# Modulation vectors in 512-column pieces, summed in fp32 straight from their accumulators, with layer 0's MLP gate row made inside the MLP

## The chip, the cores and the metric

The kernel runs on one core of a Trainium2 chip. A core has a tensor engine (PE; its weight loads are a row of their own, PEld), a vector engine (DVE), a scalar engine (ACT), GpSimd (POOL) and SyncE (SP), which in this kernel issues all DMAs. Each engine takes its instructions in the order in which the built program holds them. The metric is device time in microseconds (us), the median of the runs.

## The reference, cut to what matters

Two transformer-like layers run over 256 context tokens and 512 latent tokens (768 in all, 1024 features). Each layer starts from six modulation vectors per conditioning, one for the latent tokens and one for the context:

```
mod = silu(c) @ w_mod[l] + b_mod[l]                  # 1024 -> 6 x 1024
sh1, sc1, g1, sh2, sc2, g2 = split(mod, 6)           # and the same from c_ctx
proj = modulate(x, sh1, sc1) @ w_in[l]               # three mixers read it: attention, S5, latent attention
mix  = merge_branches(proj, ya, ys, yc)              # gated sum of the three branches, then w_out
x_mid = post_norm(x, g1 * mix, ...)
ff   = squared_relu(modulate(x_mid, sh2, sc2) @ w_up[l]) @ w_down[l]
x    = post_norm(x_mid, g2 * ff, ...)
```

Vectors 0, 1, 3 and 4 (the shifts and scales) are used with features on partitions ("columns"); vectors 2 and 5 (the gates g1 and g2) multiply token rows and are used as "rows" of 1024 values. In the last layer the context needs vectors 0 and 1 alone.

## The kernel before, in words

All matrices are fp32. A large product is made of three fp32r matmuls on split operands (L163 to L165): the weights arrive by DMA (`wr`), ACT rounds them to a high part (`wh`, L147), and DVE, for some POOL, makes the low part (`wl`, L120 or L150).

The stages of layer 0, by the trace's time: modulation vectors 0 and 1 and the first norm (0 to 85 us), projections (85 to 416), attention and S5 (416 to 820), merge of the branches (820 to about 980), then the tail: `w_out` and the norms (to about 1105), the MLP (to about 1660) and the last norm (to 1720). Layer 1 follows to 2812 us.

The modulation vectors are made beside this work by the generator `mods`. For a piece of n columns it streams eight 128-row blocks of `w_mod` (tile `wm`), and DVE multiplies each by one value of silu(c) per partition and adds it to an accumulator (`acc`, L308 for the first, L310 for the others), one accumulator per conditioning. The accumulator still has to be summed over its 128 partitions. For this ACT rounds it to a high part (`mh`, L320), POOL makes the low part (`ml`, L321), and PE multiplies both with ones (`mod_sum`, L337) in the single PSUM bank of the pool "bg", which the S5 tables (L584, L600) share. A row vector then goes through ACT (L341) and a DMA to the DRAM array `modr`; it comes back by `gate_rows` as a broadcast tile `bc`, 128 partitions by 1024 values. The sums of a piece are issued after the last product of the piece that follows it.

There are three calls: beside layer 0's projections vectors 2, 3 and 4 in pieces of 256 columns; beside layer 0's merge vector 5, the gate of the MLP, in pieces of 128 columns, of which the context's products are made by ACT (L304) and added by POOL (L306); and beside layer 0's MLP all six vectors of layer 1 in pieces of 256, mixed with the making of layer 1's S5 tables (`s5_tables`).

In the MLP, `up_proj` makes one block of 128 hidden features (its square comes from POOL, L1228, its low part from DVE, L120), eight blocks to a group, four groups. Six of the first group's blocks are begun early, for the first 384 tokens alone. Then `proj_add` multiplies a group with `w_down`, 256 output columns at a time, for the six token tiles in turn: 24 matmuls into one of the five PSUM banks of the pool "mm", then DVE multiplies by the gate (`tmp`, L1202, reading the `bc` tile) and POOL adds to the residual (L1203). A bank is free again when `tmp` has read it.

What sets the order: each generator's steps are paced by weights (`mixed`), `later` gives a step a lower priority, and a list scheduler then fixes one order for each engine. Buffers are few: two `wm` tiles and two accumulators of each name in the MLP, so that a load waits until the tile two loads before it has been used, and an accumulator is cleared (L291) only when its earlier content has gone out.

## Time and profile before

| What | us |
|---|---|
| median of three runs | 2805.99 (2805.65 to 2811.1) |
| span of the profiled execution | 2812.2 |
| PE busy in it | 2613.1 (93%) |
| DVE busy | 1887.2 (67%) |
| ACT busy | 1285.3 (46%) |
| POOL busy | 1243.2 (44%) |
| mean granted clock of PE | 0.963 |

The page gives no separate run time for the profiled execution; its span is 6.2 us above the median and 1.1 us above the highest of the three runs. Windows of the trace give each engine's busy time for a stretch; a stretch's length less PE's busy time is the time in which PE stood still.

### The profile page before, as it was taken

What the parts mean: (1) busy time and instruction counts of PE and PEld (TensorE: products, weight loads), DVE (VectorE), ACT (ScalarE), POOL (GpSimd) and SP (SyncE); (2) the same over time, 40 slices, a digit from 0 to 9 for tenths busy, and PEclk for the clock granted to TensorE, in tenths of its full rate; (3) what the DMA queues carried; (4) which work ended last, traced back from release to release, by engine and by line L of the source; (5) the groups of instructions that cost most, each with busy time, mean ns of one, the idle gap of its engine ahead of it and who ended that gap; (6) DMA issues with size and microseconds to landing.
All of it is one profiled execution on the core that took longest, in us unless ns stands there. A gap on an engine that the chain in (4) does not pass through costs nothing.

```text
span 2812.2 us, 51061 instructions
## 1 busy us (share of the span) xinstructions
PE 2613.1 (93%) x18616; PEld 2521.8 (90%) x18616; DVE 1887.2 (67%) x3736; ACT 1285.3 (46%) x2692; POOL 1243.2 (44%) x1912
## 2 busy tenths in 40 slices
PE   7989998999999898999999988998998999799998
PEld 4988887989899797999998988997988989799997
DVE  7898856766688968467788574465766766843446
ACT  4343458555664435232322334466755643533332
POOL 2587211880113767455455362220586006722225
PEclk9989999999999999999999998999999999899999
DMA  7555766334544554244544255457433556532333
GB/s 238 168 163 153 198 195 180 96 102 122 158 135 136 165 174 143 89 131 140 157 125 133 83 159 157 120 154 199 124 102 109 147 159 210 143 103 85 91 98 113
DMA packets 509803, 397.87 MB, mean 141 GB/s; under 512 B 101424, under 2 KB 463216, under 8 KB 509552
## 3 DMA queue, kind: packets, MB, share of 16 engines
q1 hardware_dynamic: 509552, 394.61, 47.7%
q8 instruction: 146, 2.39, 0.4%
q14 instruction: 105, 0.86, 0.1%
HBM read 328.97 MB, written 70.67 MB: 142 GB/s over the span
## 4 chain that ended last, share of the span: by engine, by line
PE 53%; POOL 16%; DVE 13%; DMA 8%; issue 6%; ACT 5%; SPq 1%; POOLq 0%; DVEq 0%; ACTq 0%
PE b L164 15%; PE b L165 15%; PE b L163 15%; DVE acc L310 3%; POOL slots L1042 3%; POOL sc L1041 2%; POOL sc L1039 2%; DVE wl L120 2%; POOL sc L1040 2%; PE sc L876 2%; DMA wm<-w_mod 2%; POOL acc L1203 1%; PE b L895 1%; DMA m<-Md 1%; PE b L1072 1%
## 5 line engine op out<-in xcount | busy, mean ns | idle before, releaser
L147 ACT CAST wh<-wr 128x512 fp32r<-128x512 f32 (+1 forms) x680 | 414.5, 618 | 614.4 <-PE b L165 284.3
L163 PE MATMUL b<-h,wh 128*128 128x384 f32 (+1 forms) x2112 | 671.6, 319 | 20.6 <-ACT h L396 8.8
L165 PE MATMUL b<-h,wl 128*128 128x384 f32 (+1 forms) x2112 | 666.5, 317 | 9.0 <-DVE wl L120 8.9
L164 PE MATMUL b<-h,wh 128*128 128x384 f32 (+1 forms) x2112 | 666.9, 316 | 6.6 <-POOL h L397 5.8
L120 DVE TENSOR_TENSOR wl<-wr,wh 128x512 fp32r<-128x512 f32 x620 | 480.3, 783 | 222.5 <-ACT wh L147 216.7
L164 PE MATMUL b<-wl,a 128*128 128x256 f32 x1780 | 504.0, 287 | 15.5 <-DVE wl L120 12.1
L165 PE MATMUL b<-wh,a 128*128 128x256 f32 x1780 | 501.9, 286 | 0.0
L163 PE MATMUL b<-wh,a 128*128 128x256 f32 x1780 | 490.8, 288 | 9.6 <-DVE tmp L1202 5.4
L163 PEld LDWEIGHTS b<-h,wh 128*128 128x128 f32 x2112 | 408.3, 194 | 24.6 <-ACT h L396 10.2
L165 PEld LDWEIGHTS b<-h,wl 128*128 128x128 f32 x2112 | 407.2, 193 | 14.5 <-DVE wl L120 13.9
L164 PEld LDWEIGHTS b<-h,wh 128*128 128x128 f32 x2112 | 408.0, 193 | 9.7 <-POOL h L397 7.6
L164 PEld LDWEIGHTS b<-wl,a 128*128 128x128 f32 x1780 | 344.6, 194 | 19.8 <-DVE wl L120 15.8
L163 PEld LDWEIGHTS b<-wh,a 128*128 128x128 f32 x1780 | 336.8, 194 | 11.6 <-DVE tmp L1202 6.4
L165 PEld LDWEIGHTS b<-wh,a 128*128 128x128 f32 x1780 | 344.6, 194 | 0.3 <-DVE a L125 0.3
L1203 POOL TENSOR_TENSOR acc<-acc,tmp 128x256 f32<-128x256 f32 x200 | 177.4, 890 | 248.2 <-DVE tmp L1202 227.8
L310 DVE SCALAR_TENSOR_TENSOR acc<-wm,silu,acc 128x256 f32<-128x256 f32 (+1 forms) x472 | 265.5, 582 | 27.0 <-DMA wm<-w_mod 12.1
L1228 POOL TENSOR_TENSOR sq<-r 128x384 f32<-128x384 f32 (+1 forms) x128 | 109.1, 853 | 225.0 <-ACT r L1226 221.6
L898 DVE TENSOR_TENSOR pt<-b,pt 128x512 fp32r<-128x512 f32 x208 | 142.1, 686 | 66.6 <-ACT pt L897 65.1
L1202 DVE TENSOR_TENSOR tmp<-b,bc 128x256 f32<-128x256 f32 x200 | 82.2, 417 | 145.4 <-PE b L165 127.0
L879 DVE TENSOR_REDUCE mx<-sc 128x1 f32<-128x768 f32 (+1 forms) x160 | 133.7, 845 | 40.3 <-PE sc L876 39.3
L164 PE MATMUL b<-a,wh 128*128 128x384 f32 (+2 forms) x480 | 152.5, 322 | 1.6 <-DVE a L120 1.6
L165 PE MATMUL b<-a,wl 128*128 128x384 f32 (+2 forms) x480 | 152.1, 322 | 0.0
(385 smaller groups left out, 5418.5 us busy)
## 6 DMA issues: line engine op xcount, KB each, us to landing
wr<-w_in SPq DMA_DIRECT2D x84, 512.0 KB
wr<-w_up SPq DMA_DIRECT2D x76, 512.0 KB
wr<-w_down SPq DMA_DIRECT2D x76, 512.0 KB
wm<-w_mod SPq DMA_DIRECT2D x64, 512.0 KB
wm<-w_mod SPq DMA_DIRECT2D x64, 256.0 KB
wr<-w_out SPq DMA_DIRECT2D x28, 512.0 KB
gd<-sg SPq DMA_DIRECT2D x48, 192.0 KB
sg<-gd SPq DMA_DIRECT2D x24, 384.0 KB
```

Of the source, the lines that this page charges most:

```text
L120: self.nc.vector.tensor_tensor(out=out, in0=src, in1=hi, op=ALU.subtract)
L147: self.nc.scalar.copy(h, raw[:, j0:j0 + jj])
L163: mm(ps, lhsT=a[0], rhs=b[0], start=start, stop=False)
L164: mm(ps, lhsT=a[0], rhs=b[1], start=False, stop=False)
L165: mm(ps, lhsT=a[1], rhs=b[0], start=False, stop=stop)
L310: i = nc.vector.scalar_tensor_tensor(out=acc, in0=w, scalar=s, in1=acc, op0=ALU.mult, op1=ALU.add)
L879: nc.vector.reduce_max(out=mx, in_=sc[:, 0:nkey], axis=AX.X, negate=True)
L898: nc.vector.tensor_tensor(out=lo, in0=ps, in1=hi, op=ALU.subtract)
L1042: tt(out=nxt, in0=nxt, in1=t1, op=ALU.add)
L1202: nc.vector.tensor_tensor(out=tmp, in0=ps, in1=g[1 if t < 2 else 0][:, cs], op=ALU.mult)
L1203: nc.gpsimd.tensor_tensor(out=r[t][:, cs], in0=r[t][:, cs], in1=tmp, op=ALU.add)
L1228: nc.gpsimd.tensor_tensor(out=sq, in0=rl, in1=rl, op=ALU.mult)
```

## The change

The whole of `mods` now works in pieces of 512 columns; where a DMA brought two 128-row blocks of 256 columns it brings one of 512, and where it brought four it brings two, so that a DMA carries as many bytes as before. There is no rounding to a high and a low part: `mod_sum` multiplies the fp32 accumulators themselves with ones. For a row vector that is one matmul with 512 columns for each conditioning, for a column vector four matmuls with two columns each. The ACT and POOL path of the context's products is gone. Vector 5 of layer 0 is no longer made beside the merge. A second stream, `gate`, makes it beside the first group of the MLP, two steps to each `up_proj`, and `gate_rows` follows it, ahead of the group's `w_down`. The comments are dropped too, so the line numbers shift: L310 is L304 in the new file, L337 is L320 (rows) and L329 (columns), L341 is L323, L1202 is L1189, L584 and L600 are L571 and L587, L608 is L595.

```diff
-    def mods(self, l, ms, n, pv=(), kk=4):
+    def mods(self, l, ms, kk=2):
+        nc, n = self.nc, 512
...
-                        if v in pv:
-                            first = k == 0 and not row
-                            tmp = acc if first else self.t(self.hip, [P, n], F32, "mt")
-                            nc.scalar.activation(tmp, w, AF.Copy, scale=s)
-                            if not first:
-                                nc.gpsimd.tensor_tensor(out=acc, in0=acc, in1=tmp, op=ALU.add)
-                        elif k == 0 and not row:
+                        if k == 0 and not row:
...
-                parts = []
-                for v, acc in zip(vecs, accs):
-                    hi, lo = (self.t(self.hip, [P, n], F32R, f"{x}{v}") for x in ("mh", "ml"))
-                    nc.scalar.copy(hi, acc)
-                    nc.gpsimd.tensor_tensor(out=lo, in0=acc, in1=hi, op=ALU.subtract)
-                    parts.append((v, acc, hi, lo))
-                finish = (l, m, h, n, b, parts)
+                finish = (l, m, h, b, list(zip(vecs, accs)))
...
+    def mod_sum(self, l, m, h, b, accs):
+        nc = self.nc
+        if m in (2, 5):
+            ps = self.bank([64, 512], which="bg")
+            for v, acc in accs:
+                nc.tensor.matmul(ps[32 * v:32 * v + 1, :], lhsT=self.ones32[:, 0:1], rhs=acc, start=True, stop=True)
+            for v, acc in accs:
+                r = slice(32 * v, 32 * v + 1)
+                nc.scalar.activation(acc[r, :], ps[r, :], AF.Copy, scale=1.0 / ALPHA)
+                self.dma(out=self.modr[l, v, m // 3:m // 3 + 1, h * 512:(h + 1) * 512], in_=acc[r, :])
+            return
+        ps = self.bank([P, 2, 4, 2], which="bg")
+        for v, acc in accs:
+            for k in range(4):
+                nc.tensor.matmul(ps[:, v, k, :], lhsT=acc[:, k * P:(k + 1) * P], rhs=self.ones32, start=True, stop=True)
...
@@ tail
-        g = self.gate_rows(rows, l, 1)
+        g = {}
...
                         f.append(self.up_proj(l, pool, rows, hT, gi * 8 + m, self.chunks(l)))
+                    if gi == 0 and not last:
+                        for _ in range(2):
+                            next(gate, None)
                     yield 1.0
+                if gi == 0:
+                    if not last:
+                        drain(gate)
+                    g.update(self.gate_rows(rows, l, 1))
...
-                work.append((self.later(mixed((self.mods(l + 1, (2, 5, 3, 4, 0, 1), 256, kk=4), 96.0),
+                gate = self.later(self.mods(l, (5,)), 300, done)
+                work.append((self.later(mixed((self.mods(l + 1, (2, 5, 3, 4, 0, 1)), 96.0),
@@ layer
-                    work.append((self.later(self.mods(0, (2, 3, 4), 256, kk=2), 1000), 48))
+                    work.append((self.later(self.mods(0, (2, 3, 4), kk=1), 1000), 48))
...
-                work = [(main, 50.0)]
-                if l == 0:
-                    self.mod_pools(c2, 2)
-                    work.append((self.later(self.mods(l, (5,), 128, (1,)), 0), 80.0))
-                merge(*work)
+                drain(main)
```

The order of the built program shows where the gate stream lands. PE, at the first `w_down` column of layer 0's MLP (`b_14742` and `b_14770` are its fifth and sixth token tile before the change):

```order
L163 MATMUL b_14742<-wh_14626,a_14504 128x256
L164 MATMUL b_14742<-wl_14627,a_14504 128x256
L165 MATMUL b_14742<-wh_14626,a_14505 128x256
L163 MATMUL b_14770<-wh_14612,a_13645 128x256
L164 MATMUL b_14770<-wl_14613,a_13645 128x256
L165 MATMUL b_14770<-wh_14612,a_13646 128x256
```

The sixth tile follows the fifth directly.

PE at the same place after the change, from just behind the last matmul of the fifth tile (`b_13994`) and one table group to the first of the sixth (`b_14022`); `acc_2967` and `acc_2968` are the gate's first 512 columns (latent, context), `acc_3036` and `acc_3037` its second, `acc_2970` is a piece of layer 1:

```order
L571 MATMUL b_13540<-ident_66,gb_13463 128x128 x4
L587 MATMUL b_13605<-cb_13548,gb_13463 128x32 x4
L320 MATMUL b_13809<-acc_2967_13216,ones_73 1x512
L320 MATMUL b_13809<-acc_2968_13217,ones_73 1x512
L571 MATMUL b_13826<-ident_66,gb_13635 128x128 x4
L320 MATMUL b_13841<-acc_2970_13228,ones_73 1x512
L320 MATMUL b_13851<-acc_3036_13518,ones_73 1x512
L320 MATMUL b_13851<-acc_3037_13519,ones_73 1x512
L587 MATMUL b_14050<-cb_13834,gb_13635 128x32 x4
L571 MATMUL b_14292<-ident_66,gb_14083 128x128 x4
L587 MATMUL b_14310<-cb_14300,gb_14083 128x32 x4
L163 MATMUL b_14022<-wh_13864,a_12875 128x256
```

The sums of both gate pieces stand between the fifth and the sixth tile.

SP's queue of DMAs at that place, after the change (`wm_13596`, `wm_13602` and those behind them are loads of `w_mod`; `acc_3026` and `acc_3036` are cleared accumulators that get their bias here):

```order
L78 DMA modr_87<-acc_2967_13216 1x512
L78 DMA modr_87<-acc_2968_13217 1x512
L78 DMA s5c_14337<-s5c 128x2x32
L78 DMA Pd_91<-pt_13816 128x512
L78 DMA Qd_92<-qt_13831 128x512
L78 DMA acc_3026_13471<-b_mod 1x512
L78 DMA modr_87<-acc_2970_13228 1x512
L78 DMA s5b_15011<-s5b 128x2x32
L78 DMA acc_3036_13518<-b_mod 1x512
L78 DMA wm_13596<-w_mod 128x2x512
L78 DMA Pd_91<-pt_14282 128x512
L78 DMA wm_13602<-w_mod 128x2x512
```

Three of the four loads of the gate's second piece stand behind the writes of its first (`wm_13596` here; `wm_13602` serves layer 1), and behind these rows come six more loads of `w_mod`, the gate's other two among them, the writes of `acc_3036` and `acc_3037`, and the two broadcast reads. Before the change this queue held the last two writes of the gate row (`acc_2780`, `acc_2781`) and its broadcast reads among the loads of `w_out`, one matrix product earlier.

More of the change, by code (lines that the diff above doesn't have):

```diff
@@ L272, in mod_pe @@
                                     in1=b[:, hs].unsqueeze(1).to_broadcast([P, 2, 4]), op=ALU.add)
-    def mods(self, l, ms, n, pv=(), kk=4):
-        nc = self.nc
+    def mods(self, l, ms, kk=2):
+        nc, n = self.nc, 512
         finish = None
@@ L315, in mods @@
                         finish = None
-                    yield n / 512.0
-                parts = []
-                for v, acc in zip(vecs, accs):
-                    hi, lo = (self.t(self.hip, [P, n], F32R, f"{x}{v}") for x in ("mh", "ml"))
-                    nc.scalar.copy(hi, acc)
-                    nc.gpsimd.tensor_tensor(out=lo, in0=acc, in1=hi, op=ALU.subtract)
-                    parts.append((v, acc, hi, lo))
-                finish = (l, m, h, n, b, parts)
+                    yield 1.0
@@ L324, in mods @@
+                finish = (l, m, h, b, list(zip(vecs, accs)))
         self.mod_sum(*finish)
-    def mod_sum(self, l, m, h, n, b, parts):
+    def mod_sum(self, l, m, h, b, accs):
         nc = self.nc
-        nb = n // P
-        row = m in (2, 5)
-        pss = self.bank([P, 2, n], which="bg")
-        for v, acc, hi, lo in parts:
-            ps = pss[:, v]
-            for k in range(1 if row else nb):
-                for a, x in enumerate((hi, lo)):
-                    o, lhsT, rhs = ((ps[0:1, :], self.ones[:, 0:1], x) if row else
-                                    (ps[:, 2 * k:2 * k + 2], x[:, k * P:(k + 1) * P], self.ones))
-                    nc.tensor.matmul(o, lhsT=lhsT, rhs=rhs, start=a == 0, stop=a == 1)
-        for v, acc, hi, lo in parts:
-            ps = pss[:, v]
-            if row:
-                nc.scalar.activation(acc[0:1, :], ps[0:1, :], AF.Copy, scale=1.0 / ALPHA)
-                self.dma(out=self.modr[l, v, m // 3:m // 3 + 1, h * n:(h + 1) * n], in_=acc[0:1, :])
-            else:
-                i = {0: 0, 1: 1, 3: 2, 4: 3}[m]
-                nc.vector.scalar_tensor_tensor(out=self.modc[:, l, v, i, nb * h:nb * (h + 1)],
-                                               in0=ps[:, 0:2 * nb:2], scalar=float(i % 2),
-                                               in1=b[:, nb * h:nb * (h + 1)], op0=ALU.add, op1=ALU.add)
@@ new lines, in mod_sum @@
+        ps = self.bank([P, 2, 4, 2], which="bg")
+        for v, acc in accs:
+            for k in range(4):
+                nc.tensor.matmul(ps[:, v, k, :], lhsT=acc[:, k * P:(k + 1) * P], rhs=self.ones32, start=True, stop=True)
+        i = {0: 0, 1: 1, 3: 2, 4: 3}[m]
+        fs = slice(4 * h, 4 * h + 4)
+        for v, _ in accs:
+            nc.vector.scalar_tensor_tensor(out=self.modc[:, l, v, i, fs], in0=ps[:, v, :, 0], scalar=float(i % 2),
+                                           in1=b[:, fs], op0=ALU.add, op1=ALU.add)
@@ L1330, in mod_pools @@
         self.wm = self.pool(ctx, "wm", wm)
-        self.accp, self.hip = self.pool(ctx, "accp", acc), self.pool(ctx, "hip", 1)
+        self.accp = self.pool(ctx, "accp", acc)
     def build(self, ctx, stop=None):
```

## The prediction, made before the result was known

> **What bounds the kernel now.** I read the busy times first, then windows by stage, then what ended PE's idle time in the stages that the change touches, then single rows of the timeline and of the chain of waits.
>
> ```profile
> PE 2613.1 (93%) x18616; PEld 2521.8 (90%) x18616; DVE 1887.2 (67%) x3736; ACT 1285.3 (46%) x2692; POOL 1243.2 (44%) x1912
> ...
> 85.00:416.00 331.00, 302.07 (x2071) 295.09 (x2072) 268.55 (x515) 139.56 (x310) 175.84 (x183) 0.95 0.61 174
> 820.00:990.00 170.00, 156.38 (x913) 151.54 (x912) 144.75 (x302) 80.16 (x178) 89.67 (x131) 0.96 0.53 163
> 2262.00:2352.00 90.00, 89.97 (x645) 85.24 (x644) 63.02 (x117) 36.93 (x68) 24.03 (x28) 0.98 0.60 182
> 1105.00:1147.00 42.00, 36.97 (x216) 35.05 (x215) 33.35 (x59) 16.83 (x33) 22.21 (x28) 1.00 0.53 161
> 1147.00:1200.00 53.00, 53.00 (x445) 52.93 (x444) 20.65 (x41) 8.73 (x16) 23.40 (x35) 1.00 0.21 66
> 1200.00:1660.00 460.00, 444.08 (x3156) 439.20 (x3155) 333.93 (x685) 134.71 (x268) 235.92 (x344) 0.99 0.45 133
> ```
>
> The columns of a window are its stretch, its length and then the busy time of PE, PEld, DVE, ACT and POOL. PE sets the time, so a change is worth what it takes from or adds to PE's idle time. That is 28.9 us in layer 0's projections, 13.6 in its merge, 5.0 while the MLP's first hidden blocks are finished, nothing at the first `w_down` columns (1147 to 1200) and 15.9 in the rest of the MLP. The third window is layer 1's merge, which has no modulation vectors beside it: PE stands still for 0.03 us of 90.
>
> **The merge, where a stream is removed.**
>
> ```profile
> PE b L337 <- ACT mh L320: 7.2, 3, 3.5
> ...
> PE b L337 <- POOL ml L321: 0.3, 1, 0.3
> ...
> 1565.84 0.79 PE b L337 x8
> ```
>
> Of the merge's 13.6 us, 7.5 are waits of the sums for the high and the low parts of the accumulators. The 32 sums themselves take 32 x 0.11 = 3.5 us of PE (0.11 from the last row, eight in 0.79 and the gap behind them; those are column sums, and row sums of 128 columns are taken as equal). At least 7.5 + 3.5 = 11 us go, at most 13.6 + 3.5 = 17. The middle is my value, since the S5 scalars of layer 1 stay on DVE here, which layer 1's own merge does not have: **-14**.
>
> **The projections, where pieces double and the split goes.** 192 products of 256 columns on DVE become 96 of 512; 24 casts on ACT and 24 subtractions on POOL go.
>
> ```profile
> L310 DVE SCALAR_TENSOR_TENSOR acc<-wm,silu,acc 128x256 f32<-128x256 f32 x408 | 234.3, 597 | 23.9 <-DMA wm<-w_mod 9.7 <-DMA acc<-b_mod 9.4 <-POOL acc L1203 0.9
> L310 DVE SCALAR_TENSOR_TENSOR acc<-wm,silu,acc x472: 339/479/1568, 87.0 to 1610.1; 128x256 f32<-128x256 f32 x137, 128x128 f32<-128x128 f32 x21
> L254 DVE SCALAR_TENSOR_TENSOR acc<-wm,silu,acc 128x512 f32<-128x512 f32 x14 | 9.8, 732 | 0.0
> L321 POOL TENSOR_TENSOR ml<-acc,mh 128x256 fp32r<-128x256 f32 x56 | 49.3, 892 | 59.0 <-ACT mh L320 54.5 <-PE b L337 3.2 <-issue 1.1
> L320 ACT CAST mh<-acc 128x256 fp32r<-128x256 f32 x56 | 22.0, 407 | 58.4 <-PE b L337 36.7 <-issue 10.6 <-DVE acc L310 8.5
> ```
>
> By mean durations DVE is freed of 96 x (2 x 0.597 - 0.732) = 44 us, POOL of 24 x 0.892 = 21 us, ACT of 10. The 44 is too high: the 14 rows of L254 ran in the set-up, the others beside a busy POOL; by L310's median of 0.479 it is 22. DVE has idle time of 62 us already in this stage, so its relief shortens the stage only where PE waits for it. The gain is at most PE's idle 28.9 us, and it could be a loss, because the scheduler's whole order is new; I put that at 5.0, PE's idle time in the stage from 1105, the nearest one in which products of `mods` and weight splits share DVE. I take **-12**, nearer the middle, because much of PE's idle time falls to single waits for other work.
>
> **The sums on PE.** A fp32 matmul shows as two records here: 16 records for the eight column sums of L268, spaced (38.5 - 36.8) / 15 = 0.113 us, so 0.23 each; 0.43 a record with 512 columns in L247, (1.88 - 0.59) / 3, where 0.59 is one record alone, so 0.86 a row sum.
>
> ```profile
> L268 PE MATMUL b<-ones,acc x16: 251/251/272, 36.8 to 38.5; 128*128 128x2 f32 x16
> ...
> 29.30 1.88 PE L247 MATMUL b<-wm,silu 128*2 128x512 f32 x4
> ```
>
> The projections' 80 old sums cost 80 x 0.11 = 8.8, the new ones 4 x 0.86 + 32 x 0.23 = 10.8: **+2**. The MLP had 112 old ones, 12.3 us, and gets 8 x 0.86 + 48 x 0.23 = 17.9; five of the row sums (4.3) fall into the stall below, so **+1** counts.
>
> [...] The trace has two records for each matmul, and the sum goes by the row.
>
> **The gate stream, where the loss is.** Follow it through the two orders shown with the change. Call X the moment at which PE ends the fifth token tile of the first `w_down` column. All five banks of the pool "mm" then hold products that wait for DVE's `tmp`, which needs the gate row in `bc`. The trace gives X before:
>
> ```profile
> 1103.17 0.88 DVE L310 SCALAR_TENSOR_TENSOR acc<-wm,silu,acc 128x256 f32<-128x256 f32 x1
> ...
> 1145.37 0.56 DVE L120 TENSOR_TENSOR a<-sq,a 128x384 fp32r<-128x384 f32 x1 [0.72 <-POOL sq L1228]
> 1147.90 0.42 DVE L1202 TENSOR_TENSOR tmp<-b,bc 128x256 f32<-128x256 f32 x1 [1.98 <-PE b L165]
> ...
> 1157.93 0.42 DVE L1202 TENSOR_TENSOR tmp<-b,bc 128x256 f32<-128x256 f32 x1 [2.46 <-PE b L165]
> ```
>
> The last row is the fifth tile: X is 1157.9, and each tile was evicted as PE ended it. After the change the products of the gate and of layer 1 that DVE meets before its last split of a hidden block (the row at 1145.37) are 28 of 512 columns, 28 x 0.732 = 20.5 us, against 20 of 256, 20 x 0.597 = 11.9. DVE is busy for 33.4 of the 42 us of that stage, so X comes some 6 us later (0 if DVE's idle time takes it, 12 if the loads of `w_mod`, now eight instead of four, hold it too): **+6**.
>
> From X the gate's second half is a chain that nothing starts earlier. The sums of its first half stand on PE behind the fifth tile, and SP has their writes to `modr` ahead of the loads. That such a write holds SP's queue is in the trace:
>
> ```profile
> SPq L78 <- ACT acc L341: 16.2, 10, 4.9
> ...
> 1338.82 3.55 DMA wm<-w_mod
> 1351.75 2.38 DMA k<-ks
> 1354.54 3.79 DMA wm<-w_mod
> ...
>   DMA bc<-modr: 4.6, 1
> ...
> 1594.65 0.44 PE b L584 x4
> 1602.08 0.81 PE b L600 x8
> ...
> L586 ACT COPY qt<-b x32: 559/587/611, 113.4 to 1622.5; 128x512 f32<-128x512 f32 x32
> L341 ACT ACTIVATE acc<-b x32: 250/313/372, 150.2 to 1328.5; 1x256 f32<-1x256 f32 x16, 1x128 f32<-1x128 f32 x16
> L291 POOL MEMSET acc<- x32: 195/302/589, 76.7 to 1299.5; 128x256 f32 x16, 128x128 f32 x16
> ```
>
> 1. The one bank of "bg" passes through table products, three sums and their ACT reads in turn: two table groups of L600 (0.8 each) and two of L584 (0.44), two copies of 0.59 and two of about 0.2, three sums of 0.86 and three reads of about 0.4: 8.2 us.
> 2. `modr` from `acc_2970` lands (2.4, as the 2 KB of `k`), POOL clears `acc_3036` (0.5), SP issues its bias and then `wm_13596`: 3.5 us. X + 11.7.
> 3. With two `wm` tiles three loads come one after another: `wm_13596`, four products, `wm_13716`, four and two products, `wm_13803`, four products. 3 x 3.6 + 14 x 0.732 = 21.0 us. X + 32.7.
> 4. Two sums and two reads, 2.5; the write to `modr`, 2.4; the broadcast read, 4.6 (the wait that this read once cost, the nearest row). The first `tmp` starts at X + 42.
>
> PE has three table groups in that time, 3 x 1.25 = 3.8 us of work that it must do anyway. **+38**. Lower bound: steps 1 and 2 hidden, 31 - 4 = 27. Upper: loads of 6.1 us as the worst `w_mod` wait of the projections, and small DMAs of 4.5 as the worst `k`:
>
> ```profile
> 304.81 6.11 DMA wm<-w_mod
> ...
> 1464.95 4.49 DMA k<-ks
> ```
>
> That is 3 x 2.5 + 2 x 2.1 more, about 50. Queued behind the waits are, on PE, all further `w_down` columns, on SP their weights, on DVE their evictions.
>
> **The rest of the MLP.** DVE has 59 us less to do if 128 pairs save 0.462 each as above (29 us by L310's median), POOL 32 x 0.892 = 29 us less, and the tables get on during the stall. PE's idle 15.9 us is the limit, 0 the other bound; its last part lies at the norms' start. **-6**. Layer 1 has no modulation vectors to make; its gate rows are read later in the queue, still ahead of all `w_down` weights: 0.
>
> **The sum.** -14 - 12 + 2 + 1 + 6 + 38 - 6 = +15 on a span of 2812.2. Added to the median of the runs, 2806, it makes **2821 us**.
>
> **The rivals.**
> - *The relief wins.* DVE and POOL, not single waits, hold PE in the projections, and all 28.9 us of idle time go. With the stall as above the total is -2; with the stall at 27 it is -13, 2793 us. It decides once the projections give more than 27 us at a stall of 38, or more than 16 at 27. For it: DVE is busy for 81% of that stage and POOL for 53%. Against: the stall is set by orders that are fixed.
> - *They cancel*: the stall near its lower bound with gains as forecast, +4, 2810 us. For it: step 1's table work may be further along than PE's order lets me see.
> - *The stall is longer*, as six loads and the tables' small DMAs crowd SP and later `w_mod` loads stand ahead of `w_down` weights: +50 and nothing from the rest of the MLP, 2839 us. Against: DMA is at 21% in the window behind X.
> - That the split stays is ruled out: the changed program holds no cast and no subtraction of an accumulator.
>
> **How the numbers follow.** Forecast 0.42, longer stall 0.20, cancelling 0.16, relief 0.22. About 0.2%, 5.6 us, is what a measurement of this kernel can tell from no change; so slower 0.62, same 0.16, faster 0.22. The range takes most of the first and last case: 2791 to 2843. The forecast's own is 2812 to 2831.
>
> **What would show it.** In the changed profile the first `tmp` of layer 0's MLP should wait about 40 us for the DMA `bc<-modr`, PE's window there should show one gap of some 36 us, and in it DVE three waits for `wm`. Layer 0's merge should lose its waits at the sums and be 11 to 17 us shorter, the projections 5 to 20. A first `tmp` that comes within 20 us of the fifth tile proves the chain wrong; projections as long as before prove that DVE did not hold them.

## The result: slower by 33 us, with the loss where it was forecast and larger than forecast

The changed kernel takes **2839.2 us** (median; 2835.4 to 2841.2), the kernel before 2805.8 us in the same comparison: a ratio of **1.0123 [1.0108, 1.0139]**, slower by 30 to 39 us. The forecast was 2821 us, +15.

To see where the time goes I cut every trace at the same points of PE's work: all its matmuls except the sums of the vectors, each counted with the usual duration of its shape, add up to a scale that all kernels share. The kernel before and the changed kernel were each profiled twice (the second profiles come from the runs before_again and after_again below), so each stage has two lengths. The cut called X lies 1.3 us ahead of the moment X itself. The stage behind it is the `w_down` product of the first group: the sixth token tile of the first column and the next columns up to a tile from the group's end (17 evictions by `tmp` in the kernel before).

| stage (us) | before | changed | difference of the means | prediction |
|---|---|---|---|---|
| set-up and projections, to 400 | 403.0, 400.0 | 391.4, 390.5 | -10.6 | -12 + 2 |
| their end, scan, attention | 426.7, 422.0 | 432.9, 428.4 | +6.3 | 0 |
| merge | 178.9, 178.0 | 168.1, 168.6 | -10.1 | -14 |
| output projection, norms, first hidden blocks | 110.6, 111.2 | 111.1, 111.1 | +0.2 | 0 |
| last hidden blocks, to X | 37.4, 37.3 | 45.2, 45.4 | +7.9 | +6 |
| X and the first group's `w_down` | 51.4, 51.4 | 106.6, 106.4 | **+55.1** | **+38** |
| rest of the MLP, norms | 519.5, 520.1 | 507.8, 508.5 | -11.7 | -6 + 1 |
| layer 1 | 1073.0, 1070.1 | 1063.8, 1069.0 | -5.2 | 0 |

The differences add up to +32, which the timed runs' 30 to 39 us hold. Here are six of the windows, with their ends at those points, of the second profile of the kernel before (columns as in the prediction, then PE's granted clock, the DMA share and GB/s):

```profile
0.00:400.00 400.00, 354.79 (x2284) 325.56 (x2285) 328.70 (x712) 172.00 (x360) 197.28 (x209) 0.95 0.63 184
400.00:822.00 422.00, 388.89 (x2606) 371.16 (x2605) 278.05 (x577) 262.33 (x589) 149.02 (x398) 0.97 0.45 136
822.00:1000.00 178.00, 164.86 (x1004) 160.08 (x1003) 147.03 (x308) 79.70 (x179) 99.53 (x142) 0.97 0.53 169
...
1111.30:1148.60 37.30, 36.52 (x242) 35.88 (x243) 20.80 (x41) 11.59 (x23) 13.79 (x19) 1.00 0.41 129
1148.60:1200.00 51.40, 51.40 (x432) 51.33 (x431) 24.32 (x48) 8.72 (x16) 23.23 (x35) 1.00 0.28 85
1200.00:1720.10 520.10, 489.40 (x3389) 481.15 (x3388) 378.22 (x773) 169.38 (x332) 268.45 (x371) 0.96 0.46 137
```

And the same six of the second profile of the changed kernel:

```profile
0.00:390.50 390.50, 351.44 (x2275) 322.85 (x2276) 293.89 (x605) 163.68 (x328) 184.30 (x180) 0.95 0.65 191
390.50:818.90 428.40, 394.73 (x2608) 377.32 (x2607) 277.94 (x573) 262.33 (x588) 149.62 (x392) 0.94 0.44 132
818.90:987.50 168.60, 160.60 (x972) 158.85 (x971) 119.39 (x249) 52.14 (x86) 53.71 (x53) 0.97 0.48 157
...
1098.60:1144.00 45.40, 39.02 (x242) 37.86 (x242) 28.63 (x50) 12.63 (x25) 12.17 (x15) 0.92 0.51 158
1144.00:1250.40 106.40, 67.77 (x447) 58.27 (x446) 65.33 (x131) 13.87 (x27) 52.75 (x90) 0.74 0.47 143
1250.40:1758.90 508.50, 481.84 (x3373) 474.89 (x3372) 307.36 (x577) 153.94 (x289) 229.07 (x289) 0.98 0.42 125
```

The counts of PE's matmuls show that the windows hold the same work (432 against 447 in the fifth row, where the sums and table products of the stall are the surplus). That row carries the result: 51.4 us without an idle moment of PE became 106.4 us with 38.6 of them idle, at a clock of 0.74. Two other stages show that idle time is not all that counts. In the scan and attention PE's idle time is nearly the same, 33.1 and 33.7 us (length less busy time), but the same work keeps it busy for 394.7 us in place of 388.9, at a clock of 0.94 in place of 0.97. In the rest of the MLP 4.0 of the 11.6 us gained in these two profiles are idle time; the rest is a shorter busy time, at a clock of 0.98 in place of 0.96.

The busy times of the changed kernel, from its page, with DVE, ACT and POOL each relieved by 46 to 79 us and PE's work unchanged; and all that PE waited for in its merge (second profile), where the sums' waits of the kernel before are gone:

```profile
PE 2613.7 (92%) x18576; PEld 2522.2 (89%) x18576; DVE 1808.7 (64%) x3460; ACT 1239.1 (44%) x2536; POOL 1171.0 (41%) x1756
```

```profile
PE b L164 <- DVE a L120: 3.5, 3, 2.3
PE b L163 <- DVE sg L1160: 3.2, 1, 3.2
PE b L163 <- ACT a L124: 1.3, 1, 1.3
```

The stall itself, from the timeline of the changed kernel's first profile (start, duration, engine, line, operation; in brackets the idle time ahead and what ended it):

```profile
1149.87 0.28 PE L165 MATMUL b<-wh,a 128*128 128x256 f32 x1
1149.99 0.98 PE L587 MATMUL b<-cb,gb 128*128 128x32 f32 x8
...
1153.07 0.32 DVE L595 TENSOR_TENSOR ks<-ks,k 16x32 f32<-16x32 f32 x1 [15.40 <-DMA k<-ks]
...
1156.07 1.87 PE L320 MATMUL b<-acc,ones 128*1 128x512 f32 x4 [2.33 <-ACT ks L591]
...
1163.01 0.59 ACT L323 ACTIVATE acc<-b 1x512 f32<-1x512 f32 x1 [1.96 <-PE b L320]
...
1163.92 0.75 DVE L304 SCALAR_TENSOR_TENSOR acc<-wm,silu,acc 128x512 f32<-128x512 f32 x1 [1.46 <-DMA acc<-b_mod]
...
1164.85 0.52 POOL L291 MEMSET acc<- 128x512 f32 x1 [1.25 <-DMA modr<-acc]
...
1165.40 0.23 SPq L78 DMA_DIRECT2D acc<-b_mod  x1
1166.03 0.40 SPq L78 DMA_DIRECT2D wm<-w_mod  x1
...
1169.84 2.74 DVE L304 SCALAR_TENSOR_TENSOR acc<-wm,silu,acc 128x512 f32<-128x512 f32 x4 [0.94 <-DMA wm<-w_mod]
...
1176.19 4.25 DVE L304 SCALAR_TENSOR_TENSOR acc<-wm,silu,acc 128x512 f32<-128x512 f32 x6 [1.87 <-DMA wm<-w_mod]
1182.69 1.54 DVE L304 SCALAR_TENSOR_TENSOR acc<-wm,silu,acc 128x512 f32<-128x512 f32 x2 [2.25 <-DMA wm<-w_mod]
1185.21 2.74 DVE L304 SCALAR_TENSOR_TENSOR acc<-wm,silu,acc 128x512 f32<-128x512 f32 x4 [0.99 <-DMA wm<-w_mod]
1187.39 2.48 PE L320 MATMUL b<-acc,ones 128*1 128x512 f32 x4 [24.42 <-DMA wm<-w_mod]
...
1191.72 0.35 SPq L78 DMA_DIRECT2D bc<-modr  x1
...
1198.02 0.76 DVE L1189 TENSOR_TENSOR tmp<-b,bc 128x256 f32<-128x256 f32 x2 [0.70 <-DMA bc<-modr]
1198.50 0.29 PEld L163 LDWEIGHTS b<-wh,a 128*128 128x128 f32 x1 [1.38 <-DVE tmp L1189]
```

X, the end of the fifth token tile, is 1149.99. DVE has been idle for 12 us by then, and for 15 when its next step starts: in its order a table step stands first that needs a product which PE has behind that tile. Then the four steps of the forecast follow: the bank's turns until the third sum is read (1149.99 to 1163.6, 13.6 us), `modr` written, cleared accumulator and bias until the load at 1166.03 (2.4 us), loads and products until 1187.95 (21.9 us), sums, write and broadcast read until 1198.02 (10.1 us). The first `tmp` starts at **X + 48.0**.

The load at 1166.03 had two things ahead of it that ended together: the bias of its accumulator was issued at 1165.40, behind the clearing at 1164.85, and the `wm` tile that it fills came free at 1166.0, with the second of two products of layer 1 that had themselves waited for a returned accumulator (the first is the row at 1163.92). Step 3 then runs as forecast, a load and four products (1169.84), a load and six (1176.19), a load and four (1185.21).

Behind the first `tmp` some 9 us more are lost before PE works without waits again: 7.2 us of waits (the two wait rows below) and 1.5 us of a slow clock. Rows of the same timeline, and two rows of the view of PE's waits for the same stage:

```profile
1199.10 0.42 PE L165 MATMUL b<-wh,a 128*128 128x256 f32 x1
1199.31 0.41 PE L163 MATMUL b<-wh,a 128*128 128x256 f32 x1
...
1201.87 0.28 PE L163 MATMUL b<-wh,a 128*128 128x256 f32 x1
1201.99 0.28 PE L164 MATMUL b<-wl,a 128*128 128x256 f32 x1
...
1202.99 3.00 POOL L1190 TENSOR_TENSOR acc<-acc,tmp 128x256 f32<-128x256 f32 x1
```

```profile
PE b L163 <- DVE tmp L1189: 4.3, 3, 2.5
PE b L164 <- DVE wl L120: 2.9, 3, 1.7
```

DVE and POOL, set free at the same moment, run table steps and products of layer 1 between the evictions and the weight splits of the next column (one addition on POOL took 3.0 us), and PE waits for them. From 1198.50 to 1201.87 its matmuls stand 0.21 us apart, then 0.12: 16 matmuls by 0.09 = 1.5 us for a slow clock behind the gap. By windows of this trace the granted clock was 1.00 from X to 1154.10, 0.50 from there to 1201.87 and 1.00 again from 1201.87 to 1205. In proj_512_only, below, it was 0.50 for 20 us, and PE's waits for ACT's copies there were at most 1.6 us long.

### The profile page after: what moved, and what is told of

Same layout as the page of the kernel before. It is cut to its first block, busy times and chain, and to the rows that moved or that the text cites. A ratio compares the mean times of both kernels' runs of the same rounds, so it can differ in the third digit from the quotient of the medians.

```text
span 2838.7 us, 50196 instructions
## 1 busy us (share of the span) xinstructions
PE 2613.7 (92%) x18576; PEld 2522.2 (89%) x18576; DVE 1808.7 (64%) x3460; ACT 1239.1 (44%) x2536; POOL 1171.0 (41%) x1756
## 4 chain that ended last, share of the span: by engine, by line
PE 54%; POOL 17%; DVE 11%; DMA 8%; issue 5%; ACT 4%; SPq 1%; POOLq 0%; DVEq 0%; ACTq 0%
PE b L163 15%; PE b L164 15%; PE b L165 15%; POOL slots L1029 3%; POOL sc L1028 2%; POOL sc L1026 2%; DVE wl L120 2%; POOL sc L1027 2%; DVE acc L304 2%; PE sc L863 2%; DMA wm<-w_mod 2%; POOL acc L1190 1%; SPq L78 1%; PE b L882 1%; PE b L1059 1%
## 5 line engine op out<-in xcount | busy, mean ns | idle before, releaser
L163 PE MATMUL b<-h,wh 128*128 128x384 f32 (+1 forms) x2112 | 669.2, 318 | 23.2 <-ACT wh L147 10.1
L120 DVE TENSOR_TENSOR wl<-wr,wh 128x512 fp32r<-128x512 f32 (+1 forms) x620 | 486.6, 793 | 265.1 <-ACT wh L147 258.8
L304 DVE SCALAR_TENSOR_TENSOR acc<-wm,silu,acc 128x512 f32<-128x512 f32 x236 | 191.1, 832 | 42.5 <-DMA wm<-w_mod 32.7
L1164 POOL TENSOR_TENSOR a<-a,sg 128x384 f32<-128x384 f32 (+1 forms) x64 | 66.1, 1048 | 309.5 <-DVE sg L1160 302.7
L1189 DVE TENSOR_TENSOR tmp<-b,bc 128x256 f32<-128x256 f32 x200 | 82.3, 417 | 157.1 <-PE b L165 142.5
L885 DVE TENSOR_TENSOR pt<-b,pt 128x512 fp32r<-128x512 f32 x208 | 141.9, 685 | 45.4 <-ACT pt L884 43.7
```

The costliest lines, as they stand in the source:

```text
L120: self.nc.vector.tensor_tensor(out=out, in0=src, in1=hi, op=ALU.subtract)
L163: mm(ps, lhsT=a[0], rhs=b[0], start=start, stop=False)
L304: i = nc.vector.scalar_tensor_tensor(out=acc, in0=w, scalar=s, in1=acc, op0=ALU.mult, op1=ALU.add)
L885: nc.vector.tensor_tensor(out=lo, in0=ps, in1=hi, op=ALU.subtract)
L1189: nc.vector.tensor_tensor(out=tmp, in0=ps, in1=g[1 if t < 2 else 0][:, cs], op=ALU.mult)
```

## The experiments

The diffs are cuts, against the changed kernel unless another is named. Where a run makes the gate row elsewhere (gate_back, the two gate_512 runs, gate_in_projections, gate_at_pre), the `gate` stream of the MLP goes as well. "Stage" figures come from the same cutting of the trace as in the table.

**gate_back: undo the move alone** (mods_old is the function of the kernel before).

```diff
...
-                drain(main)
+                work = [(main, 50.0)]
+                if l == 0:
+                    self.mod_pools(c2, 2)
+                    self.hip = self.pool(c2, "hip", 1)
+                    work.append((self.later(self.mods_old(l, (5,), 128, (1,)), 0), 80.0))
+                merge(*work)
...
-        g = {}
+        g = self.gate_rows(rows, l, 1)
```

> Only the gate row goes back to the merge, in its old 128-column pieces with the split; everything else is as in the changed kernel. Theory A (the gate row's late arrival at the first w_down column is the whole loss): the stall of 48 us ahead of the first tmp and the restart behind it, 56 us in all against the kernel before, and the 6 us by which the fifth tile came late, go; the 9 us that the merge had gained are given back, and up to 13 us that the rest of the MLP caught up are lost. 2839 - 62 + 9 + (0 to 13) = 2786 to 2799 us, so faster than the kernel before by 7 to 20 us. Rival B (the 512-column pieces and their fp32 sums cost time of their own, which the stall only hides): 2806 us or more.

Measured: 2794.4 us, ratio 0.9959 [0.9947, 0.9972]. The first group's `w_down` takes 51.3 us, as before the change; the merge is 178.4, as before too. Everything that the change does besides the move makes the kernel faster, by 0.4%. Rival B falls.

**no_wait: the same work, and nobody waits for it.** Layer 0's MLP multiplies by the attention's gate row, which has long been there; its own gate row is made and written, and not read.

```diff
-        g = {}
+        g, g0 = {}, None if last else self.gate_rows(rows, l, 0)
...
-                    g.update(self.gate_rows(rows, l, 1))
+                    g.update(self.gate_rows(rows, l, 1) if last else g0)
```

> As the changed kernel, with all products, sums and writes of the gate row where they are, but layer 0's MLP multiplies by layer 0's attention gate row (row 0 of modr), which is read ahead of the hidden blocks: the MLP gate row is computed and not used. Theory A: nothing waits for the gate row any more, so the 56 us go and at most the 13 us that the rest of the MLP caught up come back: 2783 to 2796 us. Rival C (the sums that stand in PE's order behind the fifth tile, and the writes to modr and loads of w_mod that stand in SP's queue ahead of the w_down weights, hold PE even when no tmp waits): a gap of 20 us or more stays, 2810 us or more.

Measured: 2792.1 us, 0.9954 [0.9938, 0.9969]. The first group's `w_down` takes 52.3 us though the loads, products, sums and writes of the gate row are still made. But they do not stand where they stood. A row of this run's timeline, the sums of the first half:

```profile
1187.72 1.03 PE L320 MATMUL b<-acc,ones 128*1 128x512 f32 x4
```

The fifth tile ends at 1148.2 here, so without the wait the built program has another order: these sums run 39 us behind it, among the later columns. The run shows that the 55 us come with `tmp`'s need of the gate row and that the work as such costs next to nothing. What rival C says of the places is not tested by it: in the changed kernel PE's longest wait is at the sums themselves (24.42 us at 1187.39), so in that order the sums' place would have held PE even without `tmp`.

**hold_layer1: both pairs of accumulators for the gate row.**

```diff
+                def after_gate():
+                    while 0 not in g:
+                        yield 1.0
+                    yield from self.mods(l + 1, (2, 5, 3, 4, 0, 1))
...
-                work.append((self.later(mixed((self.mods(l + 1, (2, 5, 3, 4, 0, 1)), 96.0),
+                work.append((self.later(mixed((after_gate(), 112.0),
```

> As the changed kernel, but layer 1's vectors start only after the gate row's last product. The gate row then has both pairs of accumulators, so its second half needs neither the sums of layer 1's first piece nor the write to modr of the first half. Theory A with its chain (the accumulators' return holds the second half's loads and products, 19 us, behind X): the products of both halves are done ahead of X, and the first tmp waits only for the bank chain, sums, write and broadcast read: about X + 20 us in place of X + 48. 2839 - 28 = 2811 us (2805 to 2818). Rival D (loads of w_mod or DVE's order, not the accumulators, make the second half late): the stall stays at 40 us or more, 2832 to 2842 us.

Measured: 2821.6 us, 1.0057 [1.0039, 1.0075]. Its timeline:

```profile
1142.01 0.98 PE L587 MATMUL b<-cb,gb 128*128 128x32 f32 x8
...
1153.12 1.87 PE L320 MATMUL b<-acc,ones 128*1 128x512 f32 x4 [0.72 <-ACT qt L573]
...
1163.13 0.76 DVE L1189 TENSOR_TENSOR tmp<-b,bc 128x256 f32<-128x256 f32 x2 [1.67 <-DMA bc<-modr]
```

X is 1142.01, the second half's sums follow 11 us later without a load between, and the first `tmp` comes at X + 21.1. The stage takes 79.8 us in place of 106.5: 27 less, as expected. So layer 1's piece, which shares the buffers, held the second half back. The run gives the gate row both accumulators, both `wm` tiles and the places in the queues at once, so it does not tell these apart. The changed kernel's rows put the accumulators' return first: both the bias at 1165.40 and the product that freed the `wm` tile had waited for it. Rival D, which puts it down to loads or DVE's order alone, is unlikely by that and not excluded. X comes earlier too: the last hidden blocks take 39 us in place of 45, without layer 1's products in DVE's order ahead of them. The time came out 4 us above its bounds because the rest of the MLP takes 518.2 us here in place of 508.2. Either its side work no longer gets ahead during a long stall, or layer 1's vectors, begun later, weigh on it; the run does not say which.

**own_bank: the sums get a PSUM bank of their own.**

```diff
-                self.psum(c2, mm=5, bg=1, tr=2)
+                self.psum(c2, mm=5, bg=1, tr=1, ms=1)
...
-            ps = self.bank([64, 512], which="bg")
+            ps = self.bank([64, 512], which="ms" if "ms" in self.ps and l + m > 2 else "bg")
```

> As the changed kernel, but the row sums of the MLP stage have a PSUM bank of their own in place of one of the two for transposes, so they don't take turns with the tables. By the prediction's step 1, which took 13.6 us in the changed kernel's profile (from 1149.99 to the last of the three sums' reads at 1163.6): the sums need only themselves and their reads, some 4 us, so the first tmp comes 8 to 10 us earlier, 2839 - 9 = 2830 us (2827 to 2833). If the chain is held by something else (the table work itself, or the loads behind it): 2836 to 2842 us.

Measured: 2859.6 us, 1.0191 [1.0176, 1.0207], some 30 us above what I expected and outside both bounds. Its timeline:

```profile
1151.64 1.03 PE L320 MATMUL b<-acc,ones 128*1 128x512 f32 x4
...
1153.99 1.02 PE L320 MATMUL b<-acc,ones 128*1 128x512 f32 x2 [0.32 <-ACT acc L323]
...
1188.00 3.16 PE L320 MATMUL b<-acc,ones 128*1 128x512 f32 x4 [2.04 <-DVE acc L304]
...
1200.82 0.76 DVE L1189 TENSOR_TENSOR tmp<-b,bc 128x256 f32<-128x256 f32 x2 [2.88 <-DMA bc<-modr]
```

The sums did come at once, within 4 us of X (1151.64). But the table groups now went between the gate row's loads and products on SP, POOL and DVE, the second half's sums came at 1188.00, 36.4 us after X (37.4 in the changed kernel), and the first `tmp` at X + 49.2. Step 1 is thus not a term that can be taken off the sum: the steps share their engines with the tables. Another stage paid for it: the one with the norms, which lost one of its two banks for transposes, took 123.8 us in place of 111.1; the rest of the difference is spread over stages in which profiles scatter.

**move_alone_old_pieces: the other part alone, on the kernel before.**

```diff
-        g = self.gate_rows(rows, l, 1)
+        g = {}
...
+                    if gi == 0 and not last:
+                        for _ in range(4):
+                            next(gate, None)
...
-                self.mod_pools(c, 2)
-                work.append((self.later(mixed((self.mods(l + 1, (2, 5, 3, 4, 0, 1), 256, kk=4), 96.0),
+                self.mod_pools(c, 2, 2, 2)
+                gate = self.later(self.mods(l, (5,), 256, kk=2), 300, done)
+                work.append((self.later(mixed((self.mods(l + 1, (2, 5, 3, 4, 0, 1), 256, kk=2), 96.0),
...
```

> The kernel before with the other part of the change alone: the gate row is made in the MLP at the same place of the program, but in 256-column pieces with the split, and layer 1's vectors keep theirs (their loads bring two row blocks at a time in place of four). Theory A (the move is the loss, the format is not): the merge saves 10 us; the first tmp waits for four pieces whose accumulators come back one behind the other, so no shorter than the changed kernel's 48 us, and the restart adds 8 to 10: 2804 - 10 + 6 + 55 = 2855 us (2840 to 2875). Rival B (the fp32 sums and long pieces make the stall): the stall is under 30 us, 2825 us or less.

Measured: 2891.5 us, 1.0313 [1.0298, 1.0327], 36 us more than I had worked out and outside the bounds of both theories; rival B, which needed a short stall, is further off. Its timeline (L337 are the sums of the split there):

```profile
1144.19 0.60 PE L584 MATMUL b<-ident,gb 128*128 128x128 f32 x4
...
1168.49 0.37 PE L337 MATMUL b<-mh,onesr 128*1 128x256 f32 x1 [18.80 <-ACT mh L320]
...
1194.44 0.37 PE L337 MATMUL b<-mh,onesr 128*1 128x256 f32 x1 [20.39 <-ACT mh L320]
...
1218.22 0.37 PE L337 MATMUL b<-mh,onesr 128*1 128x256 f32 x1 [18.64 <-ACT mh L320]
...
1227.93 0.74 DVE L1202 TENSOR_TENSOR tmp<-b,bc 128x256 f32<-128x256 f32 x2
```

Three pieces stand behind X, one every 25 us, and the first `tmp` comes at X + 83.7. With 512 columns only one piece stands there. The two parts of the change are not independent: the new format costs nothing that can be told (proj_512_only, below) and shortens the stall that the move brings. How much of that the longer pieces do, and how much the missing split, for which PE waits 18.6 to 20.4 us here, is not separated.

**proj_512_only: the new format in the projections alone, on the kernel before** (mods_new is the changed kernel's function).

```diff
-                    work.append((self.later(self.mods(0, (2, 3, 4), 256, kk=2), 1000), 48))
+                    work.append((self.later(self.mods_new(0, (2, 3, 4), kk=1), 1000), 48))
```

> The kernel before with one part of the change: the vectors beside layer 0's projections in 512-column pieces with fp32 sums, without the split; the gate row stays in the merge and layer 1's vectors stay in 256-column pieces. Theory G (from the profiles so far: PE's work stands 9 to 11 us earlier at 400 us than in the second profile of the kernel before, but only 0 to 4 us earlier where the merge starts): the gain is made in the projections and given back at the scan and the attention, so 2800 to 2804 us against about 2804. Theory of the prediction (12 us less in the projections, 2 more for the sums, and what is gained there stays): 2794 us.

Measured: 2802.2 us, 0.9994 [0.9983, 1.0005], no change that can be told. Up to 400 us it takes 389.1, some 12 less than the kernel before; scan and attention take 430.8, against 426.7 and 422.0. Two windows of this run, the second of them a part of the scan:

```profile
389.10:819.90 430.80, 395.40 (x2609) 378.23 (x2608) 279.54 (x579) 263.75 (x592) 150.16 (x399) 0.94 0.44 132
...
405.60:426.10 20.50, 15.65 (x71) 14.30 (x71) 3.84 (x10) 13.94 (x31) 0.00 (x0) 0.50 0.89 256
```

And PE's waits for the copies of the scan's inputs, in the second profile of the kernel before and then in this run (L1031 and L1094 are the same line):

```profile
PE b L1026 <- ACT slots L1031: 3.9, 6, 1.2
...
PE b L1089 <- ACT slots L1094: 9.5, 11, 1.6
```

PE comes to the scan earlier and waits there more often for ACT, though other waits shrink in turn: its idle time in the stage is 35.4 us, against 33.1 (422.00 less 388.89). The larger part of the loss is the clock. The same work keeps PE busy for 395.4 us in place of 388.9, at a clock of 0.94 in place of 0.97, and for 20 us of the scan the granted clock is 0.50, while none of PE's waits for ACT's copies there is longer than 1.6 us. Ten profiles in which the projections take 388 to 391 us have 427 to 434 us there; the four with 400 to 403 us have 422 to 427. So about half of the gain is lost again in the next stage. What brings the clock down there is not shown.

**gate_512_in_merge, gate_512_merge_later: the gate row in the merge, in the new format.**

```diff
...
-                drain(main)
+                work = [(main, 50.0)]
+                if l == 0:
+                    self.mod_pools(c2, 2, 1)
+                    work.append((self.later(self.mods(l, (5,), kk=1), 0), 16.0))
+                merge(*work)
```

The second run has 300 in place of the 0. Both have one accumulator of each name in the merge, where gate_back has two.

> As gate_back, but the gate row beside the merge is in 512-column pieces with fp32 sums too. The old pieces cost the merge 8 to 13 us by the slips of the runs without them. Theory A (the waits of the sums for the split caused most of it): two pieces with two sums each wait far less often; the merge loses 3 to 6 us in place of 10, 2787 to 2791 us. Rival H (DVE's load causes it: 32 products of 0.73 us more on a DVE that is busy for 108 of 142 us there): no better than gate_back, 2793 us or more.

> As gate_512_in_merge, but the gate row's steps are scheduled as if they came 300 instructions later, so that the merge's own work goes first. In gate_512_in_merge DVE ran 32 products from 820 to 874 us, PE waited 3.9 us for the split of a GLU tile behind them, and the merge gained only 3 of the 10 us that it gains with no vectors. Theory K (the place of the products inside the merge costs the other 6 us): 2781 to 2784 us. Theory H (DVE's load there costs them, wherever the products stand): 2785 to 2789 us, no change.

Measured: 2787.0 us, 0.9926 [0.9910, 0.9943], and 2788.3 us, 0.9942 [0.9926, 0.9958]. The merge takes 175.4 and 177.7 us, against 178.4 with the old pieces and 165 to 169 with none. Two rows of PE's waits in the merge of the first:

```profile
PE b L163 <- ACT a L124: 3.9, 1, 3.9
PE b L163 <- ACT wh L147: 3.8, 1, 3.8
```

The first run's time is the one that theory A gave, but the merge is not: it gains 3 us, not 4 to 7. No sum is waited for any more, but other work is late behind the products, and placing them later does not help: K falls, and H fits the merge of both, though its time for the first (2793 us or more) was missed. Whether the single accumulator has a part in it is not tested. The total of the first is 7 us better than gate_back, of which the merge has 3 and the rest of the MLP (509.7 against 514.8) 5; two profiles of one kernel differ by as much, so I don't divide it further.

**gate_in_projections: the gate row beside the projections.**

```diff
-        g = {}
+        g = self.gate_rows(rows, l, 1)
...
-                    work.append((self.later(self.mods(0, (2, 3, 4), kk=1), 1000), 48))
+                    work.append((self.later(self.mods(0, (2, 5, 3, 4), kk=1), 1000), 64))
```

> As gate_back, but the gate row is made beside layer 0's projections, right behind the attention gate row, in 512-column pieces; the merge has no vectors. Theory A and G (the merge saves its 10 us, DVE has 79 us of idle time in the 315 us of the projections for 32 products of 0.73 us, and what a longer projection stage loses is not lost where the merge starts): 2794 - 10 + (0 to 5) = 2784 to 2789 us. Rival I (the projections wait for DVE): they grow by the 23 us of products, 2796 us or more.

Measured: **2786.4 us, 0.9930 [0.9916, 0.9944]**, in the bounds of theory A and G. The projections take 402.0 us again, scan and attention 424.5, the merge 165.6: what the projections lose is half won back at the scan, and the merge keeps its 12 us. With gate_512_in_merge it is the best version found; both beat the kernel before by 0.7%.

**gate_at_pre: behind the merge, but 40 us earlier.**

```diff
...
+        gc = ExitStack()
+        if not last:
+            self.mod_pools(gc, 2)
+            gate = self.later(self.mods(l, (5,)), 300, done)
+        for m in range(PRE):
+            pre.append(self.up_proj(l, pool, rows, hT, m, htok[0:1]))
+            if not last:
+                for _ in range(3):
+                    next(gate, None)
...
```

> As the changed kernel (no vectors beside the merge, 512-column pieces), but the gate row is begun some 40 us earlier, beside the six hidden blocks of the first token half, and its pools are opened there; layer 1's vectors begin after it, so it has both pairs of accumulators. PE's order has its four sums in front of the last hidden blocks and the first w_down column, as far as the order shows. Theory A (only lateness at the first w_down column costs): no stall, the merge's 10 us and the MLP's 5 to 10 us stay gained, DVE's 23 us of products beside the norms and first blocks cost 0 to 6 us: 2804 - 10 - 8 + 3 = about 2789 us (2782 to 2794). Rival J (any place of the gate row behind the merge delays the hidden blocks by its DVE work, since DVE is busy for 31 of 40 us there): 23 us less 9 of idle time, about 14 us lost, 2798 us or more.

Measured: 2791.7 us, 0.9955 [0.9942, 0.9969]. The merge takes 166.2, the first group's `w_down` 56.2 in place of 106.5; the norms and hidden blocks ahead of it take 8 us more than before the change. So a place behind the merge is not wrong in itself, only one that ends behind X. Rival J falls by the time, though 8 of the 14 us that it named are lost.

**before_again, after_again: the same two kernels, for second profiles.**

> The kernel before once more, unchanged, for a second profile of it. Between the two profiles of before and after, layer 1's stages, which the change does not touch, differ by 9 us in favour of the changed kernel, and the middle of the attention by some 3 us. Theory E (that is a difference from run to run): this profile lies some 6 us under the first one, at about 2806, and its layer 1 is shorter than the first's by several us. Rival F (the change does shorten layer 1): its layer 1 agrees with the first profile's to 1 or 2 us.

> The changed kernel once more, unchanged, for a second profile. Its first profile has layer 1 some 6 us shorter than the second profile of the kernel before, though gate_back and no_wait have it equal to 2 us. Theory E (a difference from run to run): this profile's layer 1 agrees with the kernel before's to 2 or 3 us, while the merge (8 to 10 us shorter) and the stall from the fifth tile to the restart (55 us) come out again. Theory F (the change shortens layer 1): 6 us again.

Measured: 2803.9 and 2841.4 us. The first profile of the kernel before, on which the forecast was made, was 10 us longer than the second (spans 2812.2 and 2801.9), 8 of them ahead of the merge. Layer 1 takes 1069.0 us in the changed kernel's second profile, against 1070.1: theory E holds, the shorter layer 1 was a difference from run to run. Merge and stall came out alike to 0.5 us.

## Why the forecast was right in sign and wrong in size

The mechanism was right and one term of the sum was mis-sized: the gate chain, +38, which measured +55.1. That is nearly all of the difference between forecast and result. The errors of the other terms add up to +12 (merge, scan, X) and -12 (rest of the MLP, layer 1, projections), so that they cancel is luck.

- **The gate chain, +38: right mechanism, too small by 17 us.** This is the step that failed. The time to the first `tmp` was 48.0 against 42, by its steps 13.6 (8.2), 2.4 (3.5), 21.9 (21.0), 10.1 (9.5). Step 1 was short because I counted the bank's turns as engine time only (the terms that I listed add up to 7.8, not 8.2); in the trace the table copy at 1155.81 had waited 3.25 us for DVE, which itself had waited for the DMA of `k` until 1153.07. Step 3, the longest, came out by the loads and products that I had named. The largest part of the rest, some 9 us, is what I had named as "queued behind the waits" and priced at nothing: the restart, with DVE and POOL full of work that was held up as well. gate_back and no_wait show the price of the wait as a whole, hold_layer1 that of sharing the buffers with layer 1. Two of the signs also came otherwise than I had written: `tmp` itself waited for `bc` for 0.70 us only, because DVE had its products to do until then, and PE's longest gap was 24.4 us, at the sums, not 36 at the sixth tile.
- **X later, +6: right.** 7.9 us, and 2 without layer 1's products ahead of X (hold_layer1).
- **The merge, -14: mechanism right, 4 us too much.** All waits at the sums went (7.0 us of them in the second profile of the kernel before, where I had read 7.5), but others grew, for DVE's `a` and `sg`, and the lower bound of 11 us was nearest.
- **The projections, -12 + 2: right in their stage (-10.6), wrong for the time.** I ended the sum at the stage. The next one gives 6 us back, and proj_512_only as a kernel gains nothing that can be told. I had priced every stage by PE's idle time; what is lost here is mostly PE's own busy time (394.7 us in place of 388.9 in the second profiles), at a lower clock (0.94 in place of 0.97). Why the clock falls and ACT's copies are late for an earlier scan stays open.
- **The rest of the MLP, -6 + 1: -11.7.** About half of it is what gate_back and no_wait show as well (5 and 8 us); the rest may be work that got ahead during the stall, since hold_layer1, with a shorter stall, has 518.2 us there. The limit that I set, PE's idle time, left out the clock here too (0.98 in place of 0.96).
- **Layer 1, 0: right**, as after_again shows; the -5 in the table's means comes from the two first profiles.
- **Sums on PE, +2 and +1.** Too small to be told in a run; in gate_512_in_merge no sum is waited for. A fp32 record of 512 columns took 0.43 us in L247 of the kernel before, at a granted clock of 1.00, against 2 x 0.12 = 0.24 us for as many columns of the split matmuls, so the two records of one row sum, 0.86 us, take as long as 3.6 of those. The four records of two row sums took 1.03 us together in no_wait, less than the 1.72 that I counted.
- **The rivals.** "The stall is longer" gave 2839 us, the measured time, and that is luck: the stall was 55, not 50, the scan and the merge gave back a part of what it counted as gained, and the MLP, of which it expected nothing, did catch up. "The relief wins" and "they cancel" needed a stall of at most 27 us or gains of 27 us; neither came. The sentence that projections "as long as before prove that DVE did not hold them" had no case: they were shorter.

The best reading of the change: the new format is worth some 10 us (gate_back), of which the projections alone make nothing that can be told, and the place of the gate row costs some 45 (2839.2 against 2794.4).

## What to carry to other kernels

Before work is moved to a later stage, find the first consumer and count back from it what must come back first: accumulators, banks, queue places. A stall also needs a price for its end, here some 9 us, because all engines that it held wake with a backlog. A gain in one stage counts only after the next stage's waits and granted clock have been read: PE's idle time alone missed the loss here. Fewer, longer pieces of a stream are worth most where each piece waits for the return of a buffer: here 25 us a piece, with the split's waits in it.

## What the runs showed of the hardware that I had not expected

- Behind a gap PE's 256-column matmuls stood 0.21 us apart for 3.4 us, at a granted clock of 0.50, then 0.12, at 1.00; the granted clock of the whole stage was 0.74 to 0.76, in the same stage before 1.00. It was worth 1.5 us here.
- In the scan of proj_512_only the granted clock was 0.50 from 405.6 to 426.1 us, though PE was busy for 15.65 of these 20.5 us and its waits for ACT there were at most 1.6 us long.
- A PSUM bank that was taken from the transposes cost 12 to 13 us in the norms' stage (123.8 against 111.1 us), more than the 9 us that I had expected of it at the sums.
- Two profiles of one unchanged kernel differed by 5 us in the attention and by 3 to 5 us in layer 1, while the stages between the merge and X agreed to 0.9 us: differences below that need a second profile.
